# A conformer block and two attention layers on one core: the first block's transfers in a written order, low parts on VectorE, heads in pairs

## The chip, the cores and the metric

The kernel runs on one core of one Trainium2 chip. The metric is the device time of one execution in microseconds (us), the median over several executions. The kernel before has a median of 1054.85 us in 3 runs (1051.34 to 1055.1). The engines are TensorE (PE), VectorE (DVE), ScalarE (ACT), GpSimd (POOL) and SyncE (SP, which here does nothing but issue transfers).

## The reference, cut to what matters

256 tokens of 1024 features go through one conformer block and then through two transformer layers, all in fp32.

```python
def first_block(...):                                   # DEPTH = 1
    mod_l = (silu(c) @ w_mod[i] + b_mod[i])             # 1024 -> 6*1024: sh1, s1, g1, sh2, s2, g2
    hl = rms_norm(xl, norm1_g) * (1 + s1_l) + sh1_l
    u = hl @ w_pw1 + b_pw1                              # 1024 -> 2048
    a, gate = split(u); u = a * sigmoid(gate)
    u = dwconv(u in 4 segments of 64, w_dw) + b_dw      # depthwise, width 31
    yl = silu(layer_norm(u)) @ w_pw2 + b_pw2
    xl = xl + g1_l * yl
    xl = xl + g2_l * sq_relu_mlp(rms_norm(xl) * (1 + s2_l) + sh2_l, mlp_w1, mlp_w2)
    return rms_norm(xl, final_g)

def second_block(...):                                  # DEPTH_2 = 2 layers
    proj = rms_norm(h) @ w_in[i]
    # 6 MLA heads (latent, with rope), softmax
    # 5 DSA heads of 64: an indexer of 8 heads picks 64 keys of each query; softmax with a bias
    # 5 stick-breaking heads of 64: z = q k; w = exp(log_sigmoid(z) + suffix sums)
    h = h + concat(o_mla, o_dsa, o_sb) @ w_o[i]
    h = h + (silu(hf @ w_gate[i]) * (hf @ w_up[i])) @ w_down[i]
    h = h + sigmoid(rms_norm(h) @ w_ple_gate[i]) * (p[i] @ w_ple_proj[i])
```

## The kernel before

**Weights.** All weights come as one stream in the order of a list, PLAN. A matrix chunk is 128 x 1024 floats (0.5 MB); two neighbours in the list travel as one transfer of 1 MB into one of three `raw` buffers. A product in fp32 is done as three: ScalarE casts the chunk to its high part (`hi`, L413), and `lo` is the chunk less that high part, made by VectorE or, for the chunks that `_pool_lo` names, by GpSimd (L430). Both splits run two chunks ahead of their use. A `raw` buffer is free when its `lo` parts are made.

**Modulation.** The matrix `w_mod` comes in pieces of 1 MB, unsplit, each into one of four buffers called homes (`home0`, `home1`, and the two halves of the tile `home2`, which carry one name in a listing). A home is free when the piece was used. I call the pieces F (first: the columns of sh1 and s1 for a quarter of the features, two pieces each, F0 to F3), P (pairs, P0 to P7: g1 and sh2), R (one, R0 to R3: g2) and D (dots, D0 to D3: s2). F, P and R go through TensorE in `mod_chunk` (L749); their result is copied by ScalarE to `modrow` (L759) and turned into columns by matmuls (L766, L771, L776). D is multiplied and summed on VectorE in `mod_dots` (L787), against a sigmoid-weighted row of c, `czb`.

**The issue queue.** `pump` issues the stream's transfers on SP, in the order of PLAN, as far as it finds a free buffer in the program; the transfer waits on the chip until that buffer's last reader is done (L399). SP runs its queue in order, so a transfer that waits for a home holds back all behind it.

**First block.** The pw1 chunks are called c0 to c15; a chunk is 12 matmuls (L926 to L928). A quarter's modulation must be ready (M1 to M3: columns, then ScalarE's and VectorE's `modulated`) before the chunks that read it: F1 stands around c1, F2 around c4, F3 around c7, D and P in the chunks from c9 on. GLU (L883, L884), the convolution as small matmuls with constant matrices (L901, L908), the LayerNorm with transposes on TensorE (L1024) and pw2 (L705 to L707) follow. pw2 runs in two halves: four early steps among the transposes, each with one R piece behind it, then `finish()` for the rest. The taps are summed into `wf` at the start (L816).

**Attention.** While the 18 chunks of the in-projection (`in`, PSUM tile `g_ps`) and then those of MLA and of `wo` run on TensorE, a generator `heads()` is stepped between them. It starts one head at a time from a list and moves all live heads one step on; at most five are live. A stick-breaking head has scores `z_ps` (L1429, L1430), then ScalarE, VectorE, TensorE (L1443 to L1445) in turn, then `value_out`. A softmax head has `s_ps` (L1392, L1393). Heads of 64 features use 64 of TensorE's 128 rows; two neighbours lie on different halves. The bias sums of the five DSA heads, `bn`, are made by GpSimd (L1360).

Of the kernel before, what the change touches and what calls it, by code (L numbers as in the profile page):

```python
# [41 lines left out]
PW1_EARLY = 9  # L42

PW1_MODS = {1: 1, 4: 2, 7: 3}
# [4 lines left out]
def _plan():  # L49
# [21 lines left out]
    first(0)  # L71
    pw1(0)
    first(1)
    pw1(1, 2, 3)
    first(2)
    pw1(4, 5)
    first(3)
    pw1(6, 7, 8, 9)
    for n in range(3):
        mod("dots", 4, n)  # L80
        mod("pair", 2, n)
        pw1(10 + 2 * n, 11 + 2 * n)
    mod("dots", 4, 3)
    mod("pair", 2, 3)
    pw2(0, 1)
    for k in range(4, 8):
        mod("pair", 2, k)
    mod("one", 5, 0)
    pw2(2, 3)
    for j in range(1, 4):  # L90
        mod("one", 5, j)
    pw2(4, 5, 6, 7)
# [38 lines left out]
def _pool_lo(key):  # L131

    name, i = key[0], key[2]
    return name == "pg" or (name == "in" and i >= 8 and i % 2 == 0) or (name == "wo" and i >= 4)
# [347 lines left out]
def tile_conformer_then_mixer(ctx: ExitStack, tc: tile.TileContext, stream, xT, pT, vec, con, rows_in, taps, c_row, out):  # L482
# [25 lines left out]
    nc.scalar.dma_start(cons[:, :CON_FIRST], con[:, :CON_FIRST])  # L508
    nc.scalar.dma_start(rows1[:32, :D], taps)
    nc.sync.dma_start(h, xT)  # L510
    nc.gpsimd.dma_start(rows1[32:33, :], rows_in[:, : 2 * D])
# [43 lines left out]
    def slot():  # L555
        step(stages)
        step(bg)
# [235 lines left out]
    ln_exp()  # L793
# [5 lines left out]
    nc.vector.tensor_copy(b_hi, b_in)  # L799
    nc.vector.tensor_sub(b_lo, b_in, b_hi)  # L800
    accA = tp.tile([P, T], F32, tag="accA", name="accA")
    nc.scalar.activation(accA, h[:, 0, :], AF.Square)
    parts = []
    for k in range(1, KB):
        if k < KB - 1:
            s = square(h[:, k, :])
            nc.vector.tensor_add(accA, accA, s)
        else:
            parts = [square(h[:, k, :]), accA]
    rbc = tp.tile([P, T], F32, tag="rbc", name="rbc")  # L810
    G1 = cp.tile([P, KB], F32, name="G1")


    for c in range(2):
        ps = bank("wf_ps")
        nc.tensor.matmul(ps[:RANK], C("at")[:TAPS], rows1[:TAPS, 512 * c : 512 * c + 512], start=True, stop=True)  # L816
        nc.vector.tensor_copy(wf[:RANK, 512 * c : 512 * c + 512], ps[:RANK])

# [13 lines left out]

    for q in range(2):
        pw1_bias(q)
    ps = col_sum(*parts)
    rsqrt_(rbc, ps, 1.0 / D)
    nc.scalar.preload_act_table_set("sigmoid_and_others")
# [12 lines left out]

    work = quarter(0)
    pw1_bias(2)
    W.hi(W.at)
    normed(0, 2)
    W.rest(W.at)
    for _ in work:
        pass

# [18 lines left out]
    nc.gpsimd.dma_start(czb, c_row.to_broadcast([P, D]))  # L877
# [56 lines left out]

    for i in range(PW1_EARLY):
        c = PW1_MODS.get(i)
        if c is not None:
            work = quarter(c)
        pw1_chunk(i)
        if c is not None:  # L940
            for _ in work:
                pass
            modulated(c)
        if i == 5:
            nc.scalar.activation(u[:, 0, :], czb, AF.Sigmoid)
        elif i == 6:
            nc.vector.tensor_mul(czb, czb, u[:, 0, :])
    for i in range(PW1_EARLY, 16):
        pw1_chunk(i)
        if i == PW1_EARLY:  # L950
            nc.gpsimd.dma_start(cons[:, CON_FIRST:], con[:, CON_FIRST:])
            pTs0 = embedding(0)
        if i % 2 == 0:
            mod_chunk("pair", 2, i // 2 - 5)
        else:
            mod_dots(4, i // 2 - 4)
    mod_chunk("pair", 2, 3)
    later = list(range(4, 8))
    while bg:
        slot()  # L960
        if later:
            mod_chunk("pair", 2, later.pop(0))
    nc.vector.tensor_add(mods[:, 4, :], mods[:, 4, :], V("b_mod", 4 * KB, KB))
    bg.append(mod_columns("pair", 2))
# [63 lines left out]
    for k in range(KB + 2):  # L1028
        if k < KB:
            ln_act(k)  # L1030
        if 0 < k <= KB:
            split(xs, k - 1, acts[k - 1])
        if k > 1:
            slot()
        if k == 2:
            drain()
            nc.vector.tensor_mul(gb, mods[:, 2, :], V("b_pw2"))
        if k > 1:
            nc.scalar.activation(h[:, k - 2, :], h[:, k - 2, :], AF.Identity, bias=gb[:, k - 2 : k - 1])
        j = k - 2  # L1040
        if j in PW2_EARLY:
            pw2.step()
            mod_chunk("one", 5, j)
            if j == 3:
                bg.append(mod_columns("one", 5))
        if j == 4:
            bg.append(bias_rows())
# [113 lines left out]
    def layer(l, xs, accA, accB):  # L1161
# [120 lines left out]
        def ev_in(m, ps):  # L1282
# [14 lines left out]
            if m == 6:  # L1297
                queue.append(sb_head(1))
            if m == 8:
                queue.extend(sb_head(hh) for hh in (2, 3))  # L1300
            if m == 10:
                queue.append(sb_head(4))
# [22 lines left out]
        def indexer():  # L1325
# [33 lines left out]
            for hh in range(5):  # L1359
                nc.gpsimd.tensor_tensor(bn[:, hh, :], biasr[:, hh, :], wk, ALU.add)  # L1360
# [3 lines left out]
            queue.extend(dsa_head(hh) for hh in range(5))  # L1364
            queue.append(sb_head(0))
# [90 lines left out]
        def heads():  # L1456

            live, n = [], 0
            while len(mixed) < KB:
# [6 lines left out]
                if queue and (n % 2 == 0 or len(queue) > 2) and len(live) < 5:  # L1466
                    g = queue.pop(0)()
                    next(g)
                    live.append(g)
# [64 lines left out]
        for i in range(4):  # L1534
# [9 lines left out]
            for hh, ps in due:  # L1544
                nc.vector.tensor_mul(qT[:, hh, :], ps, rq)
                queue.append(mla_head(hh))
# [169 lines left out]
```

## Time and profile before

| | |
|---|---|
| median of 3 runs | 1054.85 us |
| the profiled execution | 1053.24 us |
| its span | 1051.5 us |
| TensorE busy | 1013.8 us (96%) |
| VectorE busy | 747.5 us (71%) |
| ScalarE busy | 591.3 us |
| GpSimd busy | 158.9 us |
| mean granted clock of TensorE | 0.982 |

The span runs from the first to the last instruction of one execution; the execution's own time is 1.7 us longer. A busy time is the sum over an engine's instructions, so a share near 100% means that the engine has next to no gaps, not that each instruction is at its best. A line number such as L749 is that of the kernel above; a line of a helper (L399, L413, L430) stands for all of its callers.

### The profile page before, as it was taken

The numbers are of one execution on the slowest core, as the hardware profiler recorded it, in microseconds if no ns is written. First come the engines' busy times: TensorE is split into PE (matmuls) and PEld (weight loads), VectorE is DVE, ScalarE is ACT, GpSimd is POOL, SyncE is SP. The second block draws the span as 40 slices with busy tenths as digits, with TensorE's granted clock in tenths as the row PEclk, the third lists the DMA queues.
The fourth block names the chain that finished last, engine by engine and source line by source line (L and its number), as shares of the span: only waits on it lengthen the run. The fifth ranks groups of instructions, "written<-read, shape, count | busy, mean of one in ns | idle before, by whom it ended". The sixth has DMA issues, their size and how long they took to land.

```text
span 1051.5 us, 16495 instructions
## 1 busy us (share of the span) xinstructions
PE 1013.8 (96%) x6388; PEld 872.9 (83%) x6388; DVE 747.5 (71%) x1419; ACT 591.3 (56%) x1067; POOL 158.9 (15%) x117
## 2 busy tenths in 40 slices
PE   6988789999999999999999999999999999999996
PEld 3654579888888988998888888998989988888896
DVE  5465257966878689848888866477887688887645
ACT  4432365734555555767555544774576765555455
POOL 0000022000014024032000002601320500000243
PEclk8999699999999999999999999999999999999998
DMA  9975738455554441425545545453333355555541
GB/s 374 380 285 212 319 109 276 161 200 201 180 181 167 175 154 62 161 95 186 200 167 194 195 171 195 146 200 130 107 145 123 127 199 196 200 181 182 199 161 41
DMA packets 28446, 192.90 MB, mean 183 GB/s; under 512 B 3383, under 2 KB 3788, under 8 KB 6992
## 3 DMA queue, kind: packets, MB, share of 16 engines
q1 hardware_dynamic: 26496, 186.94, 49.2%
q0 software_dynamic: 1104, 3.38, 1.0%
q10 hardware_dynamic: 768, 1.53, 0.4%
q8 instruction: 50, 0.82, 0.3%
q14 instruction: 28, 0.23, 0.1%
HBM read 190.78 MB, written 2.04 MB: 183 GB/s over the span
## 4 chain that ended last, share of the span: by engine, by line
PE 81%; DVE 6%; ACT 4%; DMA 1%; issue 1%; DVEq 0%; ACTq 0%
PE g_ps L643 33%; PE g_ps L644 17%; PE g_ps L636 4%; PE g_ps L637 4%; PE g_ps L638 4%; PE mx_ps L705 3%; PE mx_ps L707 3%; PE mx_ps L706 3%; DMA home<-stream 1%; PE mod_ps L749 1%; ACT hi L413 1%; PE s_ps L1393 1%; PE cs_ps L621 1%; DVE lo L430 1%; PE o_ps L1377 1%
## 5 line engine op out<-in xcount | busy, mean ns | idle before, releaser
L413 ACT CAST hi<-raw 128x1024 fp32r<-128x1024 f32 (+2 forms) x310 | 320.4, 1036 | 291.4 <-PE g_ps L643 148.2
L430 DVE TENSOR_TENSOR lo<-raw,hi 128x1024 fp32r<-128x1024 f32 (+2 forms) x276 | 344.0, 1250 | 117.7 <-ACT hi L413 117.0
L643 PE MATMUL g_ps<-xf,hi 128*128 128x512 f32 x704 | 247.3, 397 | 0.0
L644 PE MATMUL g_ps<-xf,lo 128*128 128x256 f32 x704 | 196.4, 279 | 0.0
L643 PEld LDWEIGHTS g_ps<-xf,hi 128*128 128x128 f32 x704 | 132.2, 188 | 32.1 <-DVE xf L1573 0.4
L644 PEld LDWEIGHTS g_ps<-xf,lo 128*128 128x128 f32 x704 | 132.6, 188 | 0.3
L643 PE MATMUL g_ps<-big_f,hi 128*128 128x512 f32 x352 | 124.4, 397 | 0.0
L430 POOL TENSOR_TENSOR lo<-raw,hi 128x1024 fp32r<-128x1024 f32 x34 | 81.8, 2408 | 210.9 <-ACT hi L413 167.7
L644 PE MATMUL g_ps<-big_f,lo 128*128 128x256 f32 x352 | 99.1, 281 | 0.0
L643 PE MATMUL g_ps<-big,hi 128*128 128x512 f32 x256 | 89.8, 395 | 0.0
L643 PEld LDWEIGHTS g_ps<-big_f,hi 128*128 128x128 f32 x352 | 66.1, 188 | 16.4
L644 PE MATMUL g_ps<-big,lo 128*128 128x256 f32 x256 | 71.9, 281 | 0.0
L643 PE MATMUL g_ps<-xs_h,hi 128*128 128x512 f32 x192 | 67.9, 399 | 0.0
L607 POOL TENSOR_TENSOR accP<-accP,sq 128x256 f32<-128x256 f32 x12 | 17.8, 1481 | 330.7 <-ACT sq L606 330.7
L644 PEld LDWEIGHTS g_ps<-big_f,lo 128*128 128x128 f32 x352 | 66.4, 189 | 0.0
L643 PEld LDWEIGHTS g_ps<-big,hi 128*128 128x128 f32 x256 | 48.1, 188 | 11.3
L607 POOL TENSOR_TENSOR accA<-accA,sq 128x256 f32<-128x256 f32 x12 | 10.2, 852 | 296.7 <-ACT sq L606 296.7
L644 PE MATMUL g_ps<-xs_h,lo 128*128 128x256 f32 x192 | 53.9, 281 | 0.0
L644 PEld LDWEIGHTS g_ps<-big,lo 128*128 128x128 f32 x256 | 48.2, 188 | 0.0
L643 PEld LDWEIGHTS g_ps<-xs_h,hi 128*128 128x128 f32 x192 | 36.1, 188 | 8.9
L636 PE MATMUL g_ps<-xs_l,hi 128*128 128x256 f32 x144 | 42.4, 294 | 0.0
L636 PE MATMUL g_ps<-xn,hi 128*128 128x256 f32 x144 | 42.4, 294 | 0.0
(363 smaller groups left out, 2298.3 us busy)
## 6 DMA issues: line engine op xcount, KB each, us to landing
raw<-stream SPq DMA_DIRECT2D x142, 1024.0 KB, 4.8
home<-stream SPq DMA_DIRECT2D x24, 1024.0 KB, 8.5
raw<-stream SPq DMA_DIRECT2D x4, 904.0 KB, 4.5
raw<-stream SPq DMA_DIRECT2D x4, 768.0 KB, 4.2
raw<-stream SPq DMA_DIRECT2D x2, 896.0 KB, 4.5
raw<-stream SPq DMA_DIRECT2D x2, 784.0 KB, 4.7
h<-xT SPq DMA_DIRECT2D x1, 1024.0 KB, 6.5
raw<-stream SPq DMA_DIRECT2D x2, 512.0 KB, 14.7
```

Source lines behind the costliest of these rows:

```text
L413: self.nc.scalar.copy(hi[:, : PLAN[i][1]], raw)
L430: eng.tensor_sub(lo[:, :w], raw, hi[:, :w])
L607: nc.gpsimd.tensor_add(acc, acc, s)
L621: nc.tensor.matmul(ps[:, :T], ones, part, start=(i == 0), stop=(i == len(parts) - 1))
L636: nc.tensor.matmul(ps, hi, xs[:, k, :T], start=first, stop=False)
L637: nc.tensor.matmul(ps, lo, xs[:, k, :T], start=False, stop=False)
L638: nc.tensor.matmul(ps, hi, xs[:, k, T:], start=False, stop=last)
L643: nc.tensor.matmul(ps, hi, xs[:, k, :], start=first, stop=False, skip_group_check=True)
L644: nc.tensor.matmul(ps[:, :T], lo, xs[:, k, :T], start=False, stop=last, skip_group_check=True)
L705: nc.tensor.matmul(ps, hi[:, s], xs[:, k, :T], start=first and m < 4, stop=False, **kw)
L706: nc.tensor.matmul(ps, lo[:, s], xs[:, k, :T], start=False, stop=False, **kw)
L707: nc.tensor.matmul(ps, hi[:, s], xs[:, k, T:], start=False, stop=last, **kw)
```

## The change

There are four parts.

First, the beginning is reordered. Two transfers at the start and the later ones of `czb` and of the rest of the constants change queue: the row of biases goes from GpSimd's to ScalarE's, and `c_row` and `con` go from GpSimd's to SP's, where they stand in line with the stream. One cast moves from VectorE to ScalarE, all eight squares go into one sum, the preload of the sigmoid's table goes, F0's matmuls stand ahead of the column sum, and the tap sums (`tap_sums`) stand behind c0, with their copies on ScalarE and no longer on VectorE.

Second, the order of the stream up to pw2 and the order of its use are written out as two strings, TRANSFERS and PW1_STEPS. P6, P7 and all R pieces are used ahead of the LayerNorm's transposes, and none in pw2's steps.

Third, `_pool_lo` names the chunks `pg` alone: per layer five `lo` parts of `in` and four of `wo` move to VectorE, and so do the five bias sums.

Fourth, heads of 64 features are started two at a time: (sb0, sb1), (sb2, sb3), (dsa0, dsa1), (dsa2, dsa3), (dsa4, sb4). MLA heads stay single.

```diff
+TRANSFERS = (
+    "F0 c0 F1 c1,2 c3 F2 c4,5 D0 F3 c6,7 P0 D1 c8,9 P1 D2 c10,11 P2 P3 D3 c12,13 P4 P5 c14,15 P6 P7 w0,1 R0 R1 w2,3 R2 R3 "
+    "w4,5,6,7"
+)
+PW1_STEPS = (
+    "c0 F1 c1 M1 c2 c3 F2 c4 M2 c5 D0 c6 F3 c7 M3 c8 P0 D1 c9 P1 D2 c10 P2 c11 D3 P3 c12 P4 c13 P5 c14 c15"
+)
...
-    return name == "pg" or (name == "in" and i >= 8 and i % 2 == 0) or (name == "wo" and i >= 4)
+    return name == "pg"
...
+    nc.scalar.dma_start(rows1[32:33, :], rows_in[:, : 2 * D])
+    nc.sync.dma_start(h, xT)
     nc.scalar.dma_start(rows1[:32, :D], taps)
-    nc.sync.dma_start(h, xT)
-    nc.gpsimd.dma_start(rows1[32:33, :], rows_in[:, : 2 * D])
...
-    for c in range(2):
-        ps = bank("wf_ps")
-        nc.tensor.matmul(ps[:RANK], C("at")[:TAPS], rows1[:TAPS, 512 * c : 512 * c + 512], start=True, stop=True)
-        nc.vector.tensor_copy(wf[:RANK, 512 * c : 512 * c + 512], ps[:RANK])
...
+    def tap_sums():
+
+        for c in range(2):
+            ps = bank("wf_ps")
+            nc.tensor.matmul(ps[:RANK], C("at")[:TAPS], rows1[:TAPS, 512 * c : 512 * c + 512], start=True, stop=True)
+            nc.scalar.copy(wf[:RANK, 512 * c : 512 * c + 512], ps[:RANK])
...
+    W.hi(W.at)
+    W.rest(W.at)
     work = quarter(0)
-    pw1_bias(2)
-    W.hi(W.at)
+    ps = col_sum(accA)
+    rsqrt_(rbc, ps, 1.0 / D)
     normed(0, 2)
...
+    for item in PW1_STEPS.split():
+        taken(item[0], int(item[1:]))
+        if item == "c0":
+            tap_sums()
+            nc.sync.dma_start(czb, c_row.to_broadcast([P, D]))
...
+        elif item == "c7":
+            nc.sync.dma_start(cons[:, CON_FIRST:], con[:, CON_FIRST:])
...
+    slot()
+    slot()
+    taken("P", 6)
+    taken("P", 7)
+    slot()
+    work = mod_columns("pair", 2)
+    next(work)
+    taken("R", 0)
+    taken("R", 1)
+    slot()
+    slot()
+    taken("R", 2)
+    taken("R", 3)
...
         if j in PW2_EARLY:
             pw2.step()
-            mod_chunk("one", 5, j)
-            if j == 3:
-                bg.append(mod_columns("one", 5))
...
             if m == 6:
-                queue.append(sb_head(1))
+                queue.append((sb_head(0), sb_head(1)))
             if m == 8:
-                queue.extend(sb_head(hh) for hh in (2, 3))
-            if m == 10:
-                queue.append(sb_head(4))
+                queue.append((sb_head(2), sb_head(3)))
...
-                nc.gpsimd.tensor_tensor(bn[:, hh, :], biasr[:, hh, :], wk, ALU.add)
+                nc.vector.tensor_tensor(bn[:, hh, :], biasr[:, hh, :], wk, ALU.add)
...
-            queue.extend(dsa_head(hh) for hh in range(5))
-            queue.append(sb_head(0))
+            queue.extend([(dsa_head(0), dsa_head(1)), (dsa_head(2), dsa_head(3)), (dsa_head(4), sb_head(4))])
...
-                if queue and (n % 2 == 0 or len(queue) > 2) and len(live) < 5:
-                    g = queue.pop(0)()
-                    next(g)
-                    live.append(g)
+                if queue and (n % 2 == 0 or len(queue) > 2) and len(live) + len(queue[0]) < 6:
+                    for start in queue.pop(0):
+                        g = start()
+                        next(g)
+                        live.append(g)
```

SP's queue of before from F3 to c12,13: `raw12` is c6,7, `raw13` c8,9, `home0` D0, `home1` P0, `raw16` c10,11, the two `home2` after it D1 and P1, `raw19` c12,13.

```order
L399 DMA home2_93<-stream 128x2048 x2
L399 DMA raw12_242<-stream 128x2048
L399 DMA raw13_262<-stream 128x2048
L399 DMA home0_91<-stream 128x2048
L399 DMA home1_92<-stream 128x2048
L399 DMA raw16_319<-stream 128x2048
L399 DMA home2_93<-stream 128x2048 x2
L399 DMA raw19_396<-stream 128x2048
L399 DMA home0_91<-stream 128x2048
```

The same place after, from `c_row` (`big0`): D0 and F3's first piece (`home2` twice), F3's second (`home0`), `raw13` is c6,7, then P0, D1, `raw16` c8,9, P1 and D2.

```order
L946 DMA big0_84<-c_row 128x1024
L394 DMA home2_93<-stream 128x2048 x2
L394 DMA home0_91<-stream 128x2048
L394 DMA raw13_311<-stream 128x2048
L394 DMA home1_92<-stream 128x2048
L394 DMA home2_93<-stream 128x2048
L394 DMA raw16_367<-stream 128x2048
L394 DMA home2_93<-stream 128x2048
L394 DMA home0_91<-stream 128x2048
```

D0 and D1 have moved ahead of c8,9, and a transfer that was on GpSimd's queue stands in the line.

VectorE's queue of before around the multiplication of D0 (`home0`, L787): `raw13` is c8,9, `raw16` c10,11, L780 to L871 the modulation of F3, L884 the GLU.

```order
L430 TENSOR_TENSOR lo17_414<-raw13_262,hi17_400 128x1024
L780 TENSOR_TENSOR mods_110<-mod_cols_111,vecs_80 128x2x2
L862 SCALAR_TENSOR_TENSOR G1_139<-mods_110,vecs_80 128x2
L871 TENSOR_TENSOR xs_h1_90<-big0_84,xs_h1_90 128x256 x2
L430 TENSOR_TENSOR lo20_442<-raw16_319,hi20_428 128x1024
L430 TENSOR_TENSOR lo21_458<-raw16_319,hi21_444 128x1024
L884 TENSOR_TENSOR big0_84<-g_ps_146,sg_460 128x256
L787 SCALAR_TENSOR_TENSOR home0_91,mods_110<-home0_91,big0_84 128x1024 x2
```

VectorE's queue after, around the same multiplication (L782, `home2`): `raw13` is c6,7, `raw16` c8,9, L775 to L861 the modulation of F2.

```order
L425 TENSOR_TENSOR lo15_334<-raw13_311,hi15_320 128x1024
L775 TENSOR_TENSOR mods_110<-mod_cols_111,vecs_80 128x2x2
L852 SCALAR_TENSOR_TENSOR G1_140<-mods_110,vecs_80 128x2
L861 TENSOR_TENSOR xs_h1_90<-big0_84,xs_h1_90 128x256 x2
L425 TENSOR_TENSOR lo16_362<-raw13_311,hi16_348 128x1024
L782 SCALAR_TENSOR_TENSOR home2_93,mods_110<-home2_93,big0_84 128x1024 x2
L425 TENSOR_TENSOR lo19_383<-raw16_367,hi19_369 128x1024
L425 TENSOR_TENSOR lo20_414<-raw16_367,hi20_400 128x1024
```

D0's multiplication has moved from behind the lo parts of c10,11 to behind those of c6,7 and ahead of those of c8,9.

TensorE's queue of before where the first stick-breaking head starts in layer 0 (`z_ps`), between two chunks of the in-projection (`hi_3243` and `hi_3287`).

```order
L637 MATMUL g_ps<-xs_l_2510,lo_3271 128x256
L638 MATMUL g_ps<-xs_l_2510,hi_3243 128x256
L1429 MATMUL z_ps<-big_a_2931 128x256
L1430 MATMUL z_ps<-big_a_2931 128x128
L636 MATMUL g_ps<-xs_l_2510,hi_3287 128x256
L637 MATMUL g_ps<-xs_l_2510,lo_3289 128x256
```

The same place after (the two chunks are `hi_3242` and `hi_3286`).

```order
L632 MATMUL g_ps<-xs_l_2509,lo_3270 128x256
L633 MATMUL g_ps<-xs_l_2509,hi_3242 128x256
L1432 MATMUL z_ps<-big_a_2930 128x256
L1433 MATMUL z_ps<-big_a_2930 128x128
L1432 MATMUL z_ps<-big_a_2930 128x256
L1433 MATMUL z_ps<-big_a_2930 128x128
L631 MATMUL g_ps<-xs_l_2509,hi_3286 128x256
L632 MATMUL g_ps<-xs_l_2509,lo_3320 128x256
```

Two heads' scores stand here in a row, and the next chunk follows at once; before, the second head's scores stood a chunk or more later.

## Rows read from the trace of the kernel before

**Rows 1.** The page's head: span; busy time, share and instructions of each engine.
```profile
span 1051.5 us, 16495 instructions
...
PE 1013.8 (96%) x6388; PEld 872.9 (83%) x6388; DVE 747.5 (71%) x1419; ACT 591.3 (56%) x1067; POOL 158.9 (15%) x117
```

**Rows 2.** Windows: stretch, length, busy time of each engine, granted clock, DMA share, GB/s.
```profile
0.00:50.00 50.00, 42.03 (x180) 26.61 (x184) 23.74 (x44) 24.44 (x37) 2.48 (x8) 0.93 0.97 393
...
375.00:425.00 50.00, 47.85 (x348) 42.70 (x348) 46.88 (x133) 28.67 (x59) 18.19 (x12) 1.00 0.34 114
425.00:482.00 57.00, 56.72 (x437) 51.73 (x436) 39.45 (x107) 38.45 (x91) 16.74 (x12) 1.00 0.37 130
```

**Rows 3.** Home pieces (all, then the second); SyncE's queue: waited for, total, times, longest.
```profile
DMA to landing us min/median/max: 4.9/8.5/17.0
...
L399 SPq DMA_DIRECT2D home<-stream x1: 432/432/432, 2.1 to 2.1; - x1
...
DMA to landing us min/median/max: 10.4/10.4/10.4
...
SPq L399 <- PE mod_ps L749: 52.2, 14, 11.9
...
SPq L399 <- DVE home L787: 12.0, 2, 7.5
```

**Rows 4.** Timeline of TensorE: start, duration, line, operands, idle before and releaser.
```profile
5.93 2.88 PE L816 MATMUL wf_ps<-big,cons 31*118 31x512 f32 x3 [5.93 <-DMA big<-taps]
...
15.27 2.92 PE L749 MATMUL mod_ps<-home,cz 128*32 128x512 f32 x16
...
22.01 0.79 PE L926 MATMUL g_ps<-hi,xs_h 128*128 128x512 f32 x1 [1.72 <-ACT xs_h L866]
...
27.48 1.94 PE L749 MATMUL mod_ps<-home,cz 128*32 128x512 f32 x16
...
97.69 1.92 PE L749 MATMUL mod_ps<-home,cz 128*32 128x512 f32 x16
...
114.06 1.78 PE L1024 MATMUL tr_ps<-cons,big 128*128 128x128 f32 x6 [2.42 <-DVE big L1001]
...
119.36 0.56 PE L705 MATMUL mx_ps<-xs_ln,hi 128*128 128x256 f32 x1
...
124.06 1.06 PE L749 MATMUL mod_ps<-home,cz 128*32 128x512 f32 x8
...
139.64 1.05 PE L771 MATMUL mod_cols<-cons,modrow 128*128 128x2 f32 x8
...
140.56 0.36 PE L705 MATMUL mx_ps<-xs_ln,hi 128*128 128x256 f32 x1
```

**Rows 5.** Timeline of VectorE: one lo part of a 1024-wide chunk.
```profile
19.82 1.22 DVE L430 TENSOR_TENSOR lo<-raw,hi 128x1024 fp32r<-128x1024 f32 x1 [2.73 <-ACT hi L413]
```

**Rows 6.** Timeline of TensorE: indexer pair, first stick-breaking head, one DSA head, what follows.
```profile
371.24 0.50 PE L1335 MATMUL ix_ps<-big_a 64*128 64x128 f32 x4
...
380.14 0.70 PE L1429 MATMUL z_ps<-big_a 64*128 64x256 f32 x2 [2.03 <-DVE big_a L1294]
...
408.92 0.48 PE L1392 MATMUL s_ps<-big_a 64*128 64x128 f32 x2
...
409.77 0.38 PE L636 MATMUL g_ps<-xs_l,hi 128*128 128x256 f32 x1
```

**Rows 7.** Timelines of GpSimd (the first row) and VectorE, attention of layer 0.
```profile
374.13 2.40 POOL L430 TENSOR_TENSOR lo<-raw,hi 128x1024 fp32r<-128x1024 f32 x1 [30.13 <-ACT hi L413]
...
374.21 2.74 DVE L1347 TENSOR_TENSOR big_a<-big_a,cons 128x384 f32<-128x384 f32 x1
...
404.93 0.87 DVE L1498 SCALAR_TENSOR_TENSOR h<-h,vecs,r 128x256 f32<-128x256 f32 x2
405.72 0.55 DVE L1357 TENSOR_TENSOR big_a<-big_a 128x384 f32<-128x384 f32 x1
...
407.12 3.43 DVE L1498 SCALAR_TENSOR_TENSOR h<-h,vecs,r 128x256 f32<-128x256 f32 x2
```

## What I expect of the change

> **What bounds the kernel now.** I read the page's head first: the span is 1051.5 us and TensorE is busy for 1013.8 of it, 96% [rows 1]. So time can come only from TensorE's idle 38 us and from matmuls that vanish or overlap. Next the windows [rows 2]. In the first 50 us the DMA engines are busy 97% of the time at 393 GB/s and TensorE for 42.03 us: the beginning is bound by transfers, and 1.05 MB at that rate is 2.7 us. In 375 to 425, the attention of layer 0, VectorE is busy for 46.88 of 50 us and TensorE for 47.85: VectorE has only 3.1 us left. Third, the waits of SP's queue and the landing times of the modulation pieces [rows 3]: a piece issued with nothing ahead of it lands 4.9 us later, while SP's queue, which is in order, stood 52.2 us in 14 waits for TensorE to use an earlier piece and 12.0 us in 2 waits for VectorE to do so. So the buffers, not the transfer rate alone, decide when the stream stops. Last, the timeline of TensorE [rows 4]. The reader is to see c0 at 22.01 behind F0's 16 matmuls at 15.27; c15 over when the next pieces run at 97.69; the transposes ahead of pw2 at 114.06 after an idle 2.42; the first pw2 matmul at 119.36; and the second half of pw2 at 140.56, behind four R chunks such as that at 124.06 (1.06 each).
>
> **The profiled execution and the median.** The sum is made against the profiled execution, 1053.24 us (span 1051.5 and 1.7 around it). It lies 1.6 below the median of 1054.85; I add that at the end.
>
> **The beginning.** F0's second piece lands at 2.1 + 10.4 = 12.5 [rows 3]. Its matmuls now stand ahead of the column sum, so they start near 12.6 and not at 15.27. From there to c0 it was 6.7 us; kept, c0 starts at about 19.3, 2.7 us earlier. But the tap sums now stand between c0 and F1. They are four matmuls, 2.88 us for three [rows 4]; the second sum needs the bank that the first one's copy empties, and that copy stands on ScalarE behind the casts of c1 and c2, whose data lands after 21. c0 is 12 matmuls (5.5 us from 22.01 to 27.48); 19.3 + 5.5 + 3 or less for the sums gives F1 at 26 to 27.5 against 27.48. So the 2.7 us are given back. The tap sums' old place cost nothing, as TensorE waited for F0 there anyway. The moved row and constant transfers are 0.5 and 0.85 MB; each stands in SP's line now, and I count 1.3 and 2.2 us of stream for them at the rate of rows 2, inside the holes below.
>
> **The middle.** F3's second piece needs the home that F2's first holds until TensorE has used it (37 to 41 by the same walk), so it lands 4.9 later, at 45 or after, and c6,7 behind it at 46 to 48. D0 is now asked for before F3, and its home comes free only when VectorE multiplies it: two multiplications of 128x1024, the shape of a lo and taken at its 1.22 [rows 5], queued behind the lo of c7, which I place at 55 to 57. D1 waits for that home, and c8,9 is behind D1 on SP: 57 + 4.9 + 2.7 = 62 to 65. On TensorE's side the row for M3 is copied by ScalarE only after the cast of c8, which waits for these bytes. So there is a hole of 7 to 9 us in the stream, and M3 and c8 wait with it; before, c8,9 stood ahead of D0. Behind the hole the pairs follow at 3 to 4 MB each, 8 to 11 us; I get c14,15 at 92 to 94 and the end of c15 at 106 to 110, against 97.5 or so [rows 4]. That is a loss of 9 to 12 us, of which most is hidden: before, TensorE did four P chunks and their waits between c15 and 114.06, 16.6 us in all. Now P0 to P5 are done before c15, and P6, P7, R0 to R3 (six times 1.06) lie with the rest of the convolution. I place the transposes at 115.5 to 120.5.
>
> **pw2.** The first matmul came 5.3 us after the transposes, because the columns of P came between (ScalarE's copy first). They are done earlier now: 2.5 us, so 118 to 123 against 119.36. From there to the second half it was 21.2 us [rows 4]. Four R chunks (4.2) and their columns (1.05, the row at 139.64) go out of it: 15.9. The second half starts at 134 to 139, in the middle 136.4 against 140.56: **-4.2 us** for the block, -1.5 at the walk's late end and -6.5 at its early one.
>
> **The lo parts on VectorE.** Per layer five `in` chunks, the five bias sums and four `wo` chunks move from GpSimd. In the attention VectorE gets five times 1.22 [rows 5] and five times 0.55 (the row at 405.72, same shape) [rows 7]: 8.9 us. The relief: while GpSimd made a lo from 374.13 for 2.40, a VectorE sum of that 128x384 shape took 2.74 instead of 0.55 [rows 7], and it ended 0.4 after GpSimd did; the two sums at 407.12 took 3.43 instead of 0.87. There are five such places in layer 0 (first and last shown); I sum 7.6 us. The bounds of the relief are 0 (each was slow for a reason that stays) and 7.6; I take 7.6 since the row at 374.21 ends with GpSimd's. Net +1.3, against 3.1 idle: covered. If the cover is gone it is 5.8 per layer (below). The four `wo` chunks lie in 425 to 482, where VectorE has 17 us free [rows 2].
> The Trainium skill, SBUF — State Buffer, section "SBUF: two separate sides", says that a VectorE operation with two SBUF inputs and a GpSimd operation that reads SBUF hold one port pair exclusively, so that the second blocks fully. The trace agrees with 2.74 against 0.55 [rows 7]; by that rule VectorE's net is about +1, without it +8.9.
>
> **Heads two at a time.** The indexer's rows already show a pair: four matmuls of 64 rows take 0.50, and two of the single head at 408.92 take 0.48; that head's whole score is 0.85 (to 409.77) [rows 6]. So a second head on the other 64 rows is nearly free: five pairs a layer save 5 x 0.85 = 4.3 us. The bounds are 0 and 4.3. The wait at 380.14 (2.03 for VectorE's rescale of the key) hits once a layer; the pair starts after the same instruction, with 2.2 us less of waiting for GpSimd ahead of it and one more lo of 1.22, so 1.0 is left. What stands against it: VectorE is nearly full there, so the heads' later steps come late, and near the end the order shows value matmuls with no projection between them, where TensorE waits: I give back 2.8 in layer 0, where the residual also runs on VectorE, and 1.3 in layer 1, both chosen and not read: 4.3 + 1.0 less these is **2.5 and 4.0 us off**.
> The Trainium skill, TensorEngine Tiling (Array Packing), section "PSUM Bottleneck", warns that tiling speeds TensorE but not the emptying of PSUM, which may become the bottleneck. Here the emptying engine is VectorE at 46.88 of 50; by that rule the saving would be nothing, which is rival 3 below.
>
> **Sum.** 1053.24 - 4.2 - 2.5 - 4.0 = 1042.5; with the 1.6 it is **1044**. About 0.5%, 5.3 us, is what a measurement of this kernel tells from no change, so "faster" begins below 1049.6 and "slower" above 1060.1.
>
> **The rivals.**
> 1. The forecast as above: 45%. Its own range is 1035 to 1050.
> 2. The stream does not stop. Up to R3 it is 35 MB, at 2.7 us 94 us; c15 could end near 83, the second half of pw2 then starts 14 + 5 us earlier: 1053.24 - 19 - 6.5 + 1.6 = 1029. For it: the homes are given back in the order in which they are asked for. Against: D0 held by VectorE, and SP's 12.0 us of such waits already [rows 3]. 13%.
> 3. VectorE is the bound in the attention: half the relief (3.8) comes, 8.9 - 3.8 - 3.1 = 2.0 us over per layer, the pairs' saving goes into TensorE's waits for VectorE, and the block gives 0 to -4.2: 1054.85 + 4.0 - (0 to 4.2) = 1055 to 1059. For: 46.88 of 50. Against: rows 7. 22%.
> 4. The second head doesn't run beside the first (it waits for a bank or for the rows): the 4.3 stay, and only the shorter wait is gained, 1.0 a layer: 1054.85 - 4.2 - 2.0 = 1049. Against: the indexer's row of four. 8%.
> 5. Slower. VectorE's added work finds no relief at all: its 8.9 go against 3.1 idle, +5.8 a layer, 11.6 in all, with the block's -4.2: 1062; with the block at 0, 1066. It decides from a relief below about 1 us per layer (5.3 + 4.2 = 9.5 over two layers is 4.75 each, and 8.9 - 3.1 - 4.75 = 1.05). For: VectorE has no room, and the queue is in order, so each lo delays the next projection chunk by itself. Against: the row at 374.21. 12%.
>
> **How the numbers follow.** Faster: nearly all of case 1 (0.43), case 2 (0.13) and over half of case 4 (0.05): 0.61. Same: case 3 and the rest of 1 and 4: 0.27. Slower: case 5: 0.12. The range goes from case 2's good end, 1027, to the middle of case 3, 1057, which leaves out some two in ten.
>
> **What would show it.** In the profile after: c0 near 19 but F1 near 27; c8's first matmul after 60 and a stretch of idle DMA before it; c15 over at 106 or later, but R's matmuls all ahead of the transposes, and no R chunk of 1.06 inside pw2's early steps; the second half of pw2 at 134 to 139. In the attention: pairs of four score matmuls at 0.50, no VectorE instruction of 128x384 at 2.7, VectorE busy near 47 of 50, and the five lo at 1.22. It would be wrong if c8 starts before 55 (case 2), if TensorE's idle time in the attention grows by over 2 us with VectorE as the releaser (cases 3 and 5), or if the four score matmuls take twice 0.48.

## The result, and the profile after

The changed kernel takes 1061.43 us (median of 4 runs, 1060.35 to 1061.89) beside 1053.89 of the kernel before (4 runs, one more than in the table above): a ratio of 1.0073, 95% interval 1.0051 to 1.0095. It is slower by about 7.5 us, where 1044 was forecast. The profiled execution took 1061.67 us.

TensorE's moments in the two profiles show where the time went (each is the start of the instruction named, in us; the block's end is the column sum behind pw2, the first `cs_ps` after 100; an attention is counted from the first `v_ps` matmul of a layer to the column sum ahead of its feed-forward stage, `cs_ps<-accF`):

| | before | after | difference |
|---|---|---|---|
| c0 | 22.01 | 18.49 | -3.5 |
| F1 | 27.48 | 27.16 | -0.3 |
| F2 | 38.70 | 40.95 | +2.3 |
| F3 | 49.93 | 57.82 | +7.9 |
| end of c15 | 97.8 | 120.8 | +23.0 |
| transposes ahead of pw2 | 114.06 | 133.46 | +19.4 |
| first block's end | 155.01 | 169.91 | +14.9 |
| attention of layer 0, length | 141.14 | 139.89 | -1.3 |
| attention of layer 1, length | 144.50 | 139.67 | -4.8 |

The rest of the difference is in the feed-forward stages (-2.4 in layer 0, +2.2 in layer 1), whose instructions are the same; the last section comes back to it. So the first block lost 14.9 us and the attention gained 6.1.

The page of the kernel after, answering to [rows 1]:

```profile
span 1059.9 us, 16455 instructions
...
PE 1015.3 (96%) x6386; PEld 875.8 (83%) x6386; DVE 752.7 (71%) x1445; ACT 593.0 (56%) x1070; POOL 101.8 (10%) x86
```

The windows after, with the attention's stretch moved by the 15 us of the delay, answering to [rows 2]; the last two are of the first block:

```profile
0.00:50.00 50.00, 40.51 (x162) 23.18 (x162) 19.44 (x36) 22.56 (x34) 0.88 (x5) 0.90 0.83 326
50.00:100.00 50.00, 36.99 (x144) 21.65 (x144) 22.68 (x38) 14.86 (x24) 0.00 (x0) 0.83 0.74 295
...
390.00:440.00 50.00, 46.73 (x348) 43.45 (x348) 47.65 (x140) 28.51 (x60) 0.92 (x2) 0.93 0.33 114
440.00:497.00 57.00, 57.00 (x444) 52.08 (x443) 43.66 (x114) 40.09 (x92) 7.02 (x8) 1.00 0.37 130
...
66.00:74.00 8.00, 5.96 (x19) 5.10 (x20) 3.53 (x6) 4.39 (x7) 0.00 (x0) 0.57 1.01 425
...
133.00:146.00 13.00, 11.99 (x56) 11.32 (x57) 4.70 (x11) 6.84 (x12) 0.00 (x0) 0.53 0.03 9
```

The transfers no longer fill the first 50 us (0.83 and 326 GB/s, 0.97 and 393 before), and from 50 to 100 TensorE is busy for 36.99 us only, where it was 46.74, as the same window of the kernel before shows:

```profile
50.00:100.00 50.00, 46.74 (x213) 26.34 (x216) 31.22 (x49) 17.50 (x27) 0.00 (x0) 0.93 0.62 238
```

In the attention VectorE is as full as it was (47.65 of 50).

SP's queue after, answering to [rows 3]:

```profile
SPq L394 <- PE mod_ps L744: 54.5, 10, 13.6
...
SPq L394 <- DVE home L782: 31.5, 4, 15.4
```

It stands behind TensorE's use of a home as long as before, and behind VectorE's 31.5 us and not 12.0, 15.4 of them at one time. That one can be followed in three timelines (start, duration, line, operands, idle before and releaser). VectorE, the lo of c7 and D0:

```profile
55.32 1.22 DVE L425 TENSOR_TENSOR lo<-raw,hi 128x1024 fp32r<-128x1024 f32 x1 [0.53 <-ACT hi L408]
56.46 1.22 DVE L782 SCALAR_TENSOR_TENSOR home<-home,big 128x1024 f32<-128x1024 f32 x1
```

ScalarE, the cast of c8 and the row of F3:

```profile
66.46 1.04 ACT L408 CAST hi<-raw 128x1024 fp32r<-128x1024 f32 x1 [11.18 <-DMA raw<-stream]
67.41 0.58 ACT L754 COPY modrow<-mod_ps 128x512 f32<-128x512 f32 x1
```

TensorE, answering to [rows 4]:

```profile
18.49 0.50 PE L915 MATMUL g_ps<-hi,xs_h 128*128 128x512 f32 x1 [0.73 <-ACT xs_h L856]
...
23.31 1.11 PE L821 MATMUL wf_ps<-big,cons 31*118 31x512 f32 x2
25.10 1.38 PE L821 MATMUL wf_ps<-big,cons 31*118 31x512 f32 x2 [0.68 <-ACT big L822]
27.16 3.64 PE L744 MATMUL mod_ps<-home,cz 128*32 128x512 f32 x16 [0.68 <-ACT big L822]
...
40.95 1.92 PE L744 MATMUL mod_ps<-home,cz 128*32 128x512 f32 x16
...
53.44 0.79 PE L915 MATMUL g_ps<-hi,xs_h 128*128 128x512 f32 x1 [3.91 <-ACT xs_h L860]
...
57.82 1.92 PE L744 MATMUL mod_ps<-home,cz 128*32 128x512 f32 x16
...
68.04 1.86 PE L771 MATMUL mod_cols<-cons,modrow 128*128 128x1 f32 x8 [5.31 <-ACT modrow L754]
69.77 0.77 PE L915 MATMUL g_ps<-hi,xs_h 128*128 128x512 f32 x1
...
120.71 1.92 PE L744 MATMUL mod_ps<-home,cz 128*32 128x512 f32 x16
...
133.46 1.79 PE L1034 MATMUL tr_ps<-cons,big 128*128 128x128 f32 x6 [2.35 <-DVE big L1011]
...
135.80 0.58 PE L700 MATMUL mx_ps<-xs_ln,hi 128*128 128x256 f32 x1 [0.55 <-ACT xs_ln L569]
...
154.47 0.39 PE L700 MATMUL mx_ps<-xs_ln,hi 128*128 128x256 f32 x1
```

D0 had landed at 36.3 and was multiplied at 56.46 to 58.8; D1's transfer waited for its home until 58.86, c8,9 was issued behind it and landed at 66.4. ScalarE's queue stood on the cast of c8 for 11.18 us, with F3's row, whose matmuls were done at 59.7, behind it; TensorE waited 5.31 us more and started c8 at 69.77, at half the clock (0.57 from 66 to 74).

A smaller hole of the same kind lies one quarter earlier. D0 has the home that F3's first piece had, so F3 and c6,7 behind it are issued later. ScalarE's queue stood on the cast of c6 until 49.75, with M2's part behind it, and TensorE waited 3.91 us ahead of c6 at 53.44. With D0 behind c8,9 (experiment 1) F3 stands at 51.86 and not at 57.82.

In the attention, TensorE's first pair of heads, the first pair of DSA heads, and the wait that is new; answering to [rows 6]:

```profile
393.85 0.71 PE L1432 MATMUL z_ps<-big_a 64*128 64x256 f32 x4 [0.99 <-DVE big_a L1300]
...
420.58 0.50 PE L1395 MATMUL s_ps<-big_a 64*128 64x128 f32 x4
...
431.03 1.69 PE L1417 MATMUL pt_ps<-cons,pr 128*128 128x128 f32 x6 [1.59 <-DVE pr L1413]
```

VectorE in the same stretch, answering to [rows 7]: the sum that took 2.74 us, a moved lo, the five bias sums.

```profile
388.96 0.56 DVE L1351 TENSOR_TENSOR big_a<-big_a,cons 128x384 f32<-128x384 f32 x1
...
391.08 1.22 DVE L425 TENSOR_TENSOR lo<-raw,hi 128x1024 fp32r<-128x1024 f32 x1
...
421.67 2.43 DVE L1364 TENSOR_TENSOR big_a<-biasr,big_a 128x384 f32<-128x384 f32 x5
```

Four score matmuls cost what two did (0.71 against 0.70, 0.50 against 0.48), the wait for the key shrank from 2.03 to 0.99, and the slow sum is down to 0.56.

### The profile page after: what moved, and what is told of

Its sections match the earlier page's. It is cut to its first block, busy times and chain, and to the rows that moved or that the text cites. A ratio compares the mean times of both kernels' runs of the same rounds, so it can differ in the third digit from the quotient of the medians.

```text
span 1059.9 us, 16455 instructions
## 1 busy us (share of the span) xinstructions
PE 1015.3 (96%) x6386; PEld 875.8 (83%) x6386; DVE 752.7 (71%) x1445; ACT 593.0 (56%) x1070; POOL 101.8 (10%) x86
## 4 chain that ended last, share of the span: by engine, by line
PE 77%; DVE 8%; ACT 4%; issue 1%; DMA 1%; DVEq 0%; ACTq 0%
PE g_ps L638 33%; PE g_ps L639 17%; PE mx_ps L700 3%; PE mx_ps L702 3%; PE g_ps L631 3%; PE mx_ps L701 3%; PE g_ps L632 2%; PE g_ps L633 2%; DVE lo L425 2%; ACT hi L408 1%; PE o_ps L1380 1%; PE pt_ps L1417 1%; PE cs_ps L616 1%; DMA home<-stream 1%; DVE big_a L1358 1%
## 5 line engine op out<-in xcount | busy, mean ns | idle before, releaser
L425 DVE TENSOR_TENSOR lo<-raw,hi 128x1024 fp32r<-128x1024 f32 (+2 forms) x294 | 361.0, 1230 | 143.2 <-ACT hi L408 142.2
L638 PEld LDWEIGHTS g_ps<-big_f,hi 128*128 128x128 f32 x352 | 66.1, 188 | 16.3
L639 PEld LDWEIGHTS g_ps<-big_f,lo 128*128 128x128 f32 x352 | 66.4, 189 | 0.0
L631 PE MATMUL g_ps<-xs_l,hi 128*128 128x256 f32 x144 | 42.9, 298 | 0.0
L632 PE MATMUL g_ps<-xs_l,lo 128*128 128x256 f32 x144 | 41.7, 290 | 0.7 <-DVE lo L425 0.7
L633 PE MATMUL g_ps<-xs_l,hi 128*128 128x256 f32 x144 | 41.6, 289 | 0.0
```

Source lines behind the costliest of these rows:

```text
L425: eng.tensor_sub(lo[:, :w], raw, hi[:, :w])
L631: nc.tensor.matmul(ps, hi, xs[:, k, :T], start=first, stop=False)
L632: nc.tensor.matmul(ps, lo, xs[:, k, :T], start=False, stop=False)
L633: nc.tensor.matmul(ps, hi, xs[:, k, T:], start=False, stop=last)
L638: nc.tensor.matmul(ps, hi, xs[:, k, :], start=first, stop=False, skip_group_check=True)
L639: nc.tensor.matmul(ps[:, :T], lo, xs[:, k, :T], start=False, stop=last, skip_group_check=True)
```

## The experiments

Ten kernels ran, each timed in five rounds beside the kernel before. All start from the changed kernel unless the text says otherwise. Totals are ratios to the kernel before; places are read from one profile each.

**1. D0 behind c8,9.** Theory A says that the place of D0 makes the holes, theory B that TensorE's added work ahead of the transposes does.

```diff
-"F0 c0 F1 c1,2 c3 F2 c4,5 D0 F3 c6,7 P0 D1 c8,9 P1 D2 c10,11 ..."
+"F0 c0 F1 c1,2 c3 F2 c4,5 F3 c6,7 c8,9 D0 P0 D1 P1 c10,11 D2 ..."
-"... c4 M2 c5 D0 c6 F3 c7 M3 c8 P0 D1 c9 ..."
+"... c4 M2 c5 c6 F3 c7 M3 c8 D0 P0 D1 c9 ..."
```

> The changed kernel, but D0 is asked for behind c8,9 (F3, c6,7, c8,9, then D0, P0, D1, P1, c10,11, and so on) and multiplied behind c8. Theory A, the early D0 makes the hole: it takes the home that F3's first piece had, so F3's second waits for F2's home and c6,7 behind it (landed 49.7), and D1 then waits for D0's home and c8,9 behind it (landed 66.4). Then c6,7 lands near 42 to 45 and c8,9 near 48, c15 is over near 100 to 106 and not at 120.7, the transposes stand near 115 to 119 and not at 133.5, and the time falls by 13 to 18 us to 1043 to 1049. Theory B, TensorE's own added work ahead of the transposes (P4 to P7 and R0 to R3 between the chunks, tap sums) makes the delay: then c15 ends at 115 or later and the time stays at 1055 or above.

Measured: 1056.55 us, ratio 1.0016 (0.9998 to 1.0034). F3 stands at 51.86 and P0, behind c8, at 60.37 (74.47 in the changed kernel); the block's end is at 162.19, 7.7 earlier. But c15 ends at 113.1 and the transposes stand at 125.97. The timeline of TensorE has the next hole one step on:

```profile
60.37 1.06 PE L744 MATMUL mod_ps<-home,cz 128*32 128x512 f32 x8
...
76.19 1.94 PE L744 MATMUL mod_ps<-home,cz 128*32 128x512 f32 x8 [6.77 <-DMA home<-stream]
...
125.97 1.79 PE L1034 MATMUL tr_ps<-cons,big 128*128 128x128 f32 x6 [2.35 <-DVE big L1011]
```

Theory A holds for 14 us at c8 and half as much at the block's end. It missed by its size: c15 and the transposes are 7 us behind its ranges, 7.2 us are left at the block's end against the kernel before, and the total is the one that theory B had forecast (1055 or above).

**2. The attention's two parts alone**, on the kernel before (the third and fourth part of the diff and nothing else).

> The kernel before with the third and the fourth part alone: lo parts and bias sums on VectorE, heads two at a time. Theory A: the attention gave -1.3 us in layer 0 and -4.8 in layer 1 in the changed kernel, whatever stands ahead of it, so 1053.9 - 6 = 1048, with the first block's end at 155 as before. Rival: the attention's gain needs the first block's delay (weights that were already there), then 1053 to 1055.

Measured: 1046.63 us, ratio 0.9933 (0.9913 to 0.9953), 7 us faster. The block ends at 155.75, the attentions take 137.79 and 141.24. The gain doesn't need the delay ahead of it.

**3. Pairs, with the lo parts and bias sums back on GpSimd.**

```diff
-    return name == "pg"
+    return name == "pg" or (name == "in" and i >= 8 and i % 2 == 0) or (name == "wo" and i >= 4)
-                nc.vector.tensor_tensor(bn[:, hh, :], ...
+                nc.gpsimd.tensor_tensor(bn[:, hh, :], ...
```

> The changed kernel with the lo parts and the bias sums back on GpSimd; pairs stay. Theory A, relief and load cancel on VectorE: 1061 +-2, VectorE busy near 47 of 50 us in the attention of layer 0, sums of 2.7 us beside GpSimd's lo again. Rival, the moved lo is what the attention gains from (fewer blocked sums): 1065 or more. Rival, the lo is a load: 1057 or less.

Measured: 1064.94 us, ratio 1.0101 (1.0074 to 1.0127). This is 2 us above my range and at the edge of the first rival's (1065 or more). The attentions take 140.56 and 141.60, 282.2 in sum. VectorE's timeline has the blocked instructions again:

```profile
386.90 2.74 DVE L1351 TENSOR_TENSOR big_a<-big_a,cons 128x384 f32<-128x384 f32 x1
...
392.69 2.71 DVE L425 TENSOR_TENSOR lo<-raw,hi 128x1024 fp32r<-128x1024 f32 x1
```

and TensorE's first pair waits as the single head did before:

```profile
392.83 0.71 PE L1432 MATMUL z_ps<-big_a 64*128 64x256 f32 x4 [2.03 <-DVE big_a L1300]
```

**4. Single heads, with the lo parts on VectorE** (the fourth part of the diff undone).

> The changed kernel with heads started one at a time again; lo parts stay on VectorE. Theory A, the pairs save TensorE 4.3 us a layer less what is given back: both attentions together 5 to 7 us longer, 1066 to 1068. Rival, pairs save nothing since VectorE bounds the stretch: 1060 to 1062.

Measured: 1066.85 us, ratio 1.0119 (1.0096 to 1.0142), in my range. The attentions take 140.21 and 143.13, 283.3 in sum. Nine profiles have both parts; their sums lie from 277.5 to 281.0, and the kernel before has 285.6. That spread goes with TensorE's granted clock. Where it stays at 1.00 through the whole attention, layer 0 takes 137.76 to 137.80 (four profiles) and layer 1 139.67 to 139.70 (five); where it falls for a time, layer 0 takes 138.35 to 139.89 and layer 1 141.20 to 141.23. The kernel before and experiments 3 and 4 have 1.00 throughout, so like can be compared with like:

| clock at 1.00 throughout | layer 0 | layer 1 | sum |
|---|---|---|---|
| kernel before | 141.14 | 144.50 | 285.6 |
| lo parts and bias sums on VectorE alone (experiment 4) | 140.21 | 143.13 | 283.3 |
| pairs alone (experiment 3) | 140.56 | 141.60 | 282.2 |
| both | 137.8 | 139.7 | 277.5 |

So the pairs are worth 5.9 us over the two layers beside the moved lo parts, within the 5 to 7 that I expected, and the lo parts, with the bias sums that always moved with them, 4.7 beside the pairs; each alone gives less (3.5 and 2.3). The first three rows are one profile each. Of the totals, the interval of experiment 3 overlaps the changed kernel's (1.0051 to 1.0095), and that of experiment 4 begins where it ends.

**5. Stream and steps in the order of before, R still ahead of the transposes.**

```diff
+"F0 c0 F1 c1,2,3 F2 c4,5 F3 c6,7 c8,9 D0 P0 c10,11 D1 P1 c12,13 D2 P2 c14,15 D3 P3 w0,1 P4 P5 P6 P7 R0 w2,3 R1 R2 R3 "
...
+"c0 F1 c1 M1 c2 c3 F2 c4 M2 c5 c6 F3 c7 M3 c8 c9 D0 c10 P0 c11 D1 c12 P1 c13 D2 c14 P2 c15 D3 P3"
...
+    for k in range(4, 8):
+        slot()
+        taken("P", k)
```

> The changed kernel with the stream and the steps of pw1 in the order of before (D0 to D3 and P0 to P3 each behind the chunks, P4 to P7 behind c15); R0 to R3 still ahead of the transposes. Theory C, the four megabytes D3 and P3 to P5 that the change puts ahead of c14,15, with their matmuls and VectorE's part, delay the chain from c15 on, on top of D0's hole: c15 ends near 97 to 100 (113.0 with D0 behind c8,9 alone, 120.7 changed), but the transposes wait for R3, which lands at 118 to 122, so they stand near 121 to 124, the block ends near 157 to 159 and the time is 1048 to 1052. Theory B, the added matmuls of P and R ahead of the transposes cost it wherever they stand: the transposes stay near 126, 1053 to 1056.

Measured: 1056.62 us, ratio 0.9993 (0.9963 to 1.0022), above my range. c15 ends at 100.9, as expected, but the transposes stand at 127.27 and the block ends at 162.77, no earlier than in experiment 1. TensorE's timeline shows what stands ahead of them:

```profile
118.24 1.94 PE L744 MATMUL mod_ps<-home,cz 128*32 128x512 f32 x8 [2.96 <-DMA home<-stream]
120.10 1.98 PE L897 MATMUL c_ps<-big,cons 119*64 119x256 f32 x8
122.01 2.53 PE L744 MATMUL mod_ps<-home,cz 128*32 128x512 f32 x16
124.47 1.05 PE L761 MATMUL mod_cols<-cons,modrow 128*128 128x4 f32 x8
127.27 1.78 PE L1032 MATMUL tr_ps<-cons,big 128*128 128x128 f32 x6 [1.75 <-DVE big L1009]
```

**6. The same with R back in pw2's early steps.** The columns of P come behind the transposes again too, as in the kernel before.

```diff
...
+    bg.append(mod_columns("pair", 2))
...
             pw2.step()
+            mod_chunk("one", 5, j)
+            if j == 3:
+                bg.append(mod_columns("one", 5))
```

> As the kernel of that name, with R0 to R3 back in pw2's early steps. Theory C: the R chunks cover their own transfers there, the transposes stand near 112 to 115, the block ends at 153 to 156 and the time is 1045 to 1049. Rival, taking R out of pw2's steps is worth its 4 to 5 us wherever the stream ends: then this one is slower than the one with R early by 2 us or more.

Measured: 1049.78 us, ratio 0.9948 (0.9924 to 0.9972). The transposes stand at 116.40, the block ends at 157.80: 5.0 us earlier than with R ahead. Transposes, block and total are all 1 to 2 us above the ends of my ranges; the rival is out. Ahead of the transposes 10.9 us are gained and behind them 5.9 lost. The part of the change that I counted as its one sure gain in the block is a loss. R and P's columns moved together here, so what each of them holds back can't be told apart.

**7. The same with the tap sums at the start** (`tap_sums()` ahead of the first biases).

> As the one before, with the tap sums at the start (before TensorE's first biases) as the kernel before has them, their copies on ScalarE. Theory: the late tap sums cost F1 2 to 3 us (F1 near 24.5 and not 27.2), and with every home one step earlier the block ends 2 to 3 us earlier: 1042 to 1046. Rival, the chunks wait for transfers, not for F1: no difference of more than 1 us.

Measured: 1046.43 us, ratio 0.9897 (0.9864 to 0.9931). F1 stands at 22.70, the transposes at 110.78, the block ends at 152.00: 5.8 us earlier, twice what I expected, and 3.0 ahead of the kernel before. The end of c15 moves by as much, from 100.2 to 94.6. The total is 0.4 above my range all the same.

**8. The changed kernel with the tap sums at the start, nothing else.**

> The changed kernel with the tap sums at the start, else unchanged. Theory: F1 near 24.5, c_row and D0 are issued 2.5 us earlier, F2 near 38, F3's second piece and c6,7 2.5 us earlier, and the block by the same: 1058 to 1060. Rival: D0's multiplication and the transfers set the pace: 1061 to 1062.

Measured: 1057.25 us, ratio 1.0008 (0.9985 to 1.0032). F1 stands at 23.68, the block ends at 164.22, 5.7 us earlier, as in experiment 7. The total is 0.8 below my range and the rival is out. The late tap sums are a cost by themselves, whatever the order behind them. SyncE's timeline shows where it begins: D0's piece, which takes a home that F1 returns, is issued 4.4 us earlier than in the changed kernel, whose row is the second:

```profile
24.81 11.54 SPq L394 DMA_DIRECT2D home<-stream  x3
...
29.16 13.24 SPq L394 DMA_DIRECT2D home<-stream  x3
```

**9. D0 behind c8,9 and R in pw2** (P's columns behind the transposes again), so that only D3 and P2 to P5 ahead of c14,15 are left of the new order.

> The changed kernel with D0 behind c8,9 (as in the first experiment) and R0 to R3 back in pw2's early steps; P2 to P5 and D3 still ahead of c14,15. Theory C, c15's end sets the block's end once R is out of the way: c15 near 113, the transposes near 119 to 122 (116.4 with P and D in the order of before), the block's end near 160 to 163. Rival: the later c15 is hidden, the transposes stand at 115 to 117.5 and the block ends at 156 to 159.

Measured: 1055.37 us, ratio 1.0010 (0.9990 to 1.0031). c15 ends at 116.1 (3 later than expected), the transposes stand at 123.13, the block ends at 163.77, all just above my ranges. The order up to c15 is that of experiment 1, where it ended at 113.1; the granted clock was another (0.62 here from 94 to 103, 1.00 there).

```profile
116.09 1.92 PE L744 MATMUL mod_ps<-home,cz 128*32 128x512 f32 x16
...
123.13 1.22 PE L1023 MATMUL tr_ps<-cons,big 128*128 128x128 f32 x6 [2.35 <-DVE big L1000]
```

From c15's end to the transposes it takes 7.0 us here and 12.9 in experiment 1; from the transposes to the block's end 40.6 and 36.2. So R out of the way gives 5.9 ahead of the transposes and costs 4.4 behind them: with c15 this late, R in pw2 gains next to nothing. The rival is out.

**10. As experiment 5, with the convolution ahead of R on TensorE.**

```diff
+    drain()
     work = mod_columns("pair", 2)
     next(work)
+    for k in range(4):
+        taken("R", k)
...
```

> As the kernel with the order of before and R ahead of the transposes, but the rest of the convolution is issued ahead of R0 to R3 on TensorE, so that it doesn't stand behind them. Theory: two things cost the 5 us, the convolution's last matmuls behind R's transfers in TensorE's queue, and the transposes behind R3, which lands at 121 to 123. The first goes: the last convolution matmul near 112 to 115 (was 120.1), no wait of the transposes for VectorE, transposes at 124 to 125.5 (were 127.3), block's end near 160. Rival, only the convolution counts: transposes near 117 to 120, block's end at 153 to 156.

Measured: 1056.86 us, ratio 1.0014 (0.9999 to 1.0029). The timeline of TensorE:

```profile
109.98 1.98 PE L897 MATMUL c_ps<-big,cons 119*64 119x256 f32 x8
...
120.56 1.94 PE L744 MATMUL mod_ps<-home,cz 128*32 128x512 f32 x8 [0.56 <-DMA home<-stream]
122.42 1.87 PE L761 MATMUL mod_cols<-cons,modrow 128*128 128x4 f32 x8
126.03 1.79 PE L1028 MATMUL tr_ps<-cons,big 128*128 128x128 f32 x6 [1.74 <-DVE big L1005]
```

The convolution is done ten us earlier, yet the transposes move by 1.2 and the block's end by 0.5, less than I expected, and F1 was 1.1 earlier in this profile anyhow. So the convolution behind R cost nothing here, against the first half of my theory. The transposes stand behind the last R piece, as in experiment 5; the rival is out too. The normalization did not use its ten us either, because VectorE's queue has the sum of P's columns ahead of it, and these columns come behind R on TensorE (a kernel with P's columns ahead of R was not run):

```profile
112.43 0.43 DVE L903 BATCH_NORM_STATS2 lnstats<-c_ps 128x6 f32<-128x256 f32 x1 [0.42 <-ACT big L902]
124.33 0.17 DVE L775 TENSOR_TENSOR mods<-mod_cols,vecs 128x16 f32<-128x16 f32 x1 [11.47 <-PE mod_cols L761]
124.42 0.32 DVE L999 BATCH_NORM_AGGREGATE lnmv<-lnstats 128x2 f32<-128x18 f32 x2
```

**What the block's 14.9 us consist of.** Each end is read from one profile. Three profiles have the changed kernel's first block, and c15 ends in them at 120.3 to 121.0; but the block ends at 169.91, at 166.97 (experiment 3) and at 171.76 (experiment 4), as the granted clock is at 0.50 for a shorter or a longer time around the transposes. So a step of 3 to 5 us is sure only where c15's end shows it too. The block's ends add up along one path, from the changed kernel (169.91): D0 behind c8,9 gives 7.7 back (162.19). Then P and D in the order of before and R in pw2 give 4.4 together (157.80), though each of them alone gives nothing (162.77 and 163.77): two conditions, a late c15 and a late R3, each enough to hold the transposes back. The tap sums at the start give 5.8 (152.00); at c15's end they give 5.6 here and 5.1 in experiment 8. That leaves the 3.0 by which this kernel is better than the one before; I put it down to the rest of the new beginning (c0 at 18 and not 22, c15's end at 94.6 and not 97.8), which no run has by itself.

## Why the prediction was wrong

**The step that failed** is the end of the middle: "That is a loss of 9 to 12 us, of which most is hidden." The mechanism had been walked rightly: F1 at 26 to 27.5 (27.16), D0 multiplied at 55 to 57 (56.46), c6,7 landing at 46 to 48 (49.7), c8,9 at 62 to 65 (66.4), F3's row behind the cast of c8. From there the sizes were off, all the same way. c8 ended at 74.5 and had ended at 58.4 before. From there to the end of c15 it took 46.3 us, where it had been 39.4. I had counted c15's end from the landing of c14,15, forecast at 92 to 94; it came at 98.5, and c14 started only near 114. TensorE itself filled this stretch: it was busy for 41.5 us, 36.4 before, with three more P chunks in it (six and not three). So c15 ended at 120.8 and not 106 to 110: a loss of 23.0 us, of which 3.6 were hidden at the transposes.

Between c15 and the transposes I had left 9.5 to 10.5 of 16.3 us, and 12.7 stayed. Moving P did set room free: with R out of there, experiment 9 has 7.0. (Five P chunks had stood there, P3 to P7, and not four: the row at 97.69 [rows 4] is of 16 matmuls, two pieces.) But R took the room. Its last piece came at 129.06 in the changed kernel; P's columns stand behind it on TensorE, and the normalization behind their sum on VectorE, though the convolution had ended at 126.6:

```profile
131.14 0.17 DVE L775 TENSOR_TENSOR mods<-mod_cols,vecs 128x16 f32<-128x16 f32 x1 [6.44 <-PE mod_cols L761]
```

**pw2** was the second error. From the transposes to the second half I forecast 18.4 us and it took 21.0 (26.5 before), as TensorE came out of the wait at half the clock and kept it until about 145 (0.53 from 133 to 146); before, it had half the clock there too, until about 123. More than that, I priced R's removal from pw2 and not its arrival ahead of it. Experiments 5 and 6 have the price: where I had written -5.25 for R and its columns, the early R and P's columns with it cost 5.0 at the block's end, 10.9 ahead of the transposes less 5.9 behind them. The last R piece came at 120.5 in experiment 10, where the convolution was done at 112; in pw2's steps that wait lies beside other work.

**The tap sums.** That the 2.7 us at c0 would be given back by F1 was right (F1 at 27.16, 27.48 before). What I did not see is what the place costs: 5.7 us at the block's end, since F1's matmuls also return two homes, and the stream behind waits for them (D0 issued at 29.16, and at 24.81 with the tap sums early).

**The attention** came out near the forecast: -2.5 and -4.0 against -1.3 and -4.8 in this profile, and -3.3 and -4.8 at a granted clock of 1.00. That the sums lie so close, 6.5 and 6.1, is in part luck: what I gave back, 2.8 and 1.3, was chosen, and I had the moved lo parts at a net load of 1.3 a layer that is covered (relief 7.6 against 8.9), while beside the pairs they are a gain of 4.7 over the two layers. The blocked 2.74 us became 0.56 [rows 7] and came back with GpSimd's lo in experiment 3, so that lo was the cause. TensorE's gain from the pairs is not lost to VectorE, so rivals 3 and 4 are out; a new wait of 1.59 for VectorE, and the lower clock after it, took part of it back in layer 0.

**The rivals.** The time landed where rival 5 had put it (1062), by another mechanism: VectorE found its relief in the attention, and the loss is in the first block. None of my five cases let the block become slower; the walk had one hole in it and every case took its end for the worst. The range ended at 1057 for that reason.

## What to carry to other kernels

In a stream that is issued in order from one queue, a transfer into a buffer that an earlier piece still holds delays all that follows, so a piece must not be asked for before its reader is near; count the time from its landing to its use (20 us for D0) as time in which that buffer is lost. Work taken out of a full stretch of the busiest engine is only a gain if its new place is not ahead of a chain that waits for something else: price the arrival and not only the removal. Of two conditions that each hold the same point back, undoing one shows nothing, so undo both.

## What the runs showed of the hardware

The two halves of TensorE's rows work side by side at no cost that shows: four score matmuls of 64 rows took 0.71 us where two took 0.70.

The same short wait is not always followed by the lower clock. After the wait of 1.59 us at 431.03, shown above, the granted clock was 0.50; in the kernel with the attention's parts alone, the same instruction waited 1.62 us and the clock stayed at 1.00. Here is a window of the changed kernel, then the instruction and a window of the other:

```profile
432.00:435.00 3.00, 3.00 (x13) 2.80 (x13) 2.93 (x13) 1.17 (x5) 0.00 (x0) 0.50 0.02 5
```

```profile
417.76 1.44 PE L1411 MATMUL pt_ps<-cons,pr 128*128 128x128 f32 x6 [1.62 <-DVE pr L1407]
...
419.00:422.00 3.00, 3.00 (x26) 2.95 (x25) 2.72 (x11) 1.44 (x5) 0.00 (x0) 1.00 0.03 5
```

All nine profiles with both parts have this wait, at 1.59 to 1.62 us. In four the clock stayed at 1.00, and the attention of layer 0 took 137.76 to 137.80 us; in five it fell to 0.50 for a time, and it took 138.35 to 139.89. So the same wait can cost from 0.6 to 2.1 us more. The feed-forward stage of a layer, with the same instructions, no wait and a granted clock of 1.00, took 185.2 us in some profiles and 187.5 in most; in the kernel before it was 187.6 in layer 0 and 185.3 in layer 1, in the changed kernel the other way round. What decides it stays open.
